# Attention as one pipeline of 24 rounds instead of six units one after another

## The chip, the cores and the metric

The kernel runs on one core of one Trainium2 chip. The metric is the device time of the program in microseconds (us). Five engines work beside each other, each in its own order: TensorE (PE, matmuls and transposes, with its weight loads shown as PEld), VectorE (DVE), ScalarE (ACT), GpSimd (POOL) and SyncE (SP), which issues the DMAs.

## The reference

One decoder layer on x (1024 tokens, width 1024). Its parts: a projection `z = rmsnorm(x) @ w_in`; a dilated attention branch and an RWKV-7 branch on parts of z; a gated merge of the two; a squared-ReLU MLP; a gated per-layer embedding. The change touches the attention branch alone:

```python
ATTN_GROUPS = ((128, 1), (512, 4), (2048, 16))    # (window, dilation), 4 heads of 64 each
q = rope(qkv[:, :, 0], pos); k = rope(qkv[:, :, 1], pos); v = qkv[:, :, 2]
for g, (window, dil) in enumerate(ATTN_GROUPS):
    idx = t[:, None] - dil * j[None, :]           # keys at stride dil, causal
    s = einsum('bqhd,bqjhd->bqhj', qb, kg) * scale
    m = max(s); e = exp(s - m); den = sum(e)
    o = einsum('bqhj,bqjhd->bqhd', e, vg) / den
# the three groups are combined per head by softmax over m + log(den)
```

## The kernel before

**Staging.** All activations stand transposed (features on partitions, tokens along the row). The program runs as: norm and transpose of x; the z projection, in items of 128 output features (48 matmuls of 128x512 into two PSUM banks, called z, half h = 0 and h = 1 with 24 each); RWKV's chunked scan among these items; attention among the last of them; merge, output projection, MLP, embedding.

**The order of the work.** The order of PE's instructions is written out by a planner at build time (class `Order`). It holds a list of dense items (`sch.add`: the z items and later work) and a set of chains (`sch.spawn`: generators for RWKV and attention). `run` takes a chain step whose planned time has come, and otherwise one more dense matmul (`fill`). The planned time of each step comes from fixed costs per engine (`Engine`, `Loads`, `HOP_DMA`, `LAG`), not from the chip. PE executes the list strictly in order. While attention runs, the order of the other engines is not the planner's: the language's own scheduler sets it.

**The units.** There are six attention units: three dilations in the order 16, 4, 1 (`GORD`), each with two pairs of heads. A unit has eight query blocks of 128 tokens. Unit n needs three z items in the order q, k, v (`add_attn`). Each half of q and k is copied out of PSUM by ScalarE (tile qk, permuted by dilation); behind the second half four DMAs build the swapped copy sw, GpSimd multiplies sw by the sine table, VectorE multiplies qk by the cosine table and adds sw (`turn_back`, rows sw and qk of the profile). v is copied out (tile v) and turned by eight PE transposes into vkb (`turn`, rows av). `attn_ok` says when the planner may take a unit's z items.

**One unit before.** `attention` waits until the unit's v is turned (`("vk", n) in done`), then until q and k are planned ready, and runs `unit`. That goes by pairs of blocks: `scores` (rows sc, into banks m0 and m1), masking and maximum on VectorE (rows SB, nm), exponentials on ScalarE (rows SB); then for each block of the pair before it the transposes of the weights (rows pt, banks s1 and s2), their copy PB on VectorE, and the values (rows po, bank s3), copied out on ScalarE to OTA or OTB. Each of these steps is handed to the planner apart, with a wait on the planned end of what it needs, so z matmuls stand between them. The next unit begins when the last block's values are issued; `natural` (rows rw, rc) turns the maxima and sums of a dilation at its end, and `combine` (rows cb) weighs the three dilations.

Of the kernel before, what the change touches and what calls it, by code (L numbers as in the profile page):

```python
# [10 lines left out]
F32 = mybir.dt.float32  # L11
F32R = mybir.dt.float32r
# [7 lines left out]
T = 1024  # L20
KT = D // 128
HD = 64
DILS = (1, 4, 16)
# [13 lines left out]
LEAD, SPARE, LAG = 0.4, 0.5, 0.4  # L37
# [204 lines left out]
def layer(ctx: ExitStack, tc: tile.TileContext, x, pT, wz, wup, w_out, wff1, w_ff2, w_ple, w_pleg,  # L242
# [3 lines left out]
    sch = Order()  # L246
# [21 lines left out]
    done = set()  # L268
# [31 lines left out]
    def wait(cond):  # L300
        while not cond():
            yield 0.1
# [603 lines left out]
    A = {}  # L906
    rope_t, MD, NAT = {}, {}, {}

    def attn_ok(n, x):
        if n < 2:  # L910
            return (("S", NU - 2) in done and ("E", NU - 1) in done and ("bv", NU - 1) in done
                    and (x < 2 or n == 0 or ("vk", 0) in done and ("v", NU - 1) in done))
        return ("B", n - 2) in done and (x < 2 or ("vk", n - 1) in done)

    def add_attn(n):
        gi, hp = n // 2, n % 2
# [51 lines left out]
    def attention():  # L968
        yield from wait(lambda: ("P", NU - 1, 1) in done)
        in_turn.__exit__(None, None, None)  # L970
        sch.in_turn = False
        V.shared = False
        amask = rtile([128, 384], "amask", "ex")
        SY.dma_start(amask, cst[:, C_BAND:C_BAND + 384])
        st = rtile([128, 512], "ast", "py")

        def stat(n=4):
            c = col[0]
            col[0] += 8 * n
            return st[:, c:c + 8 * n].rearrange("p (a b) -> p a b", b=n)  # L980

        SB = rtile([128, 4, 2, 256], "SB", "BK")
        PB = rtile([128, 4, 4, 128], "PB", "UV")
        vkb = rtile([128, 2, 8, 128], "vkb", "BT")

        def turn(n):
            yield from wait(lambda: 2 in A[n])
            yield sch.until(A[n]["t"])
            for b in range(2):
                ps, tag = yield from chain_bank([128, 4, 128], "av", ("s1", "s2"))  # L990
                for i in range(4):
# [3 lines left out]
            done.add(("vk", n))  # L995

        yield from turn(0)
        OTA = rtile([128, 2, 2, T], "OTA", "TM0")
        OTB = rtile([128, 2, 2, T], "OTB", "TM1")
        OT = {g: (OTA[:, 0], OTA[:, 1], OTB[:, 0])[i] for i, g in enumerate(GORD)}  # L1000
        for n in range(6):
            g, hp = GORD[n // 2], n % 2
            if hp == 0:
                MD[g] = stat(8)
            yield from wait(lambda: ("vk", n) in done)
            if n < 5:
                sch.spawn(turn(n + 1), 2)
            yield from wait(lambda: len(A[n].get("qk", ())) == 2)
            yield sch.until(max(A[n]["qk"]))
            if n == 5:  # L1010
                sraw = rtile([128, 768], "sraw", "v")
                SY.dma_start(sraw, cst[:, C_SEL:C_SEL + 768])
            yield from unit(n, g, hp, OT[g][:, hp], vkb[:, n % 2], SB, PB, amask)
            if n > 3:
                load_or(5 - n, G)
            if n == 5:
                load_or(2, G)
                load_or(3, V)
            if hp:
                NAT[g] = yield from natural(g, stat)  # L1020
        sel = rtile([128, 6, 128], "sel", "px", F32R)
        V.tensor_copy(sel.rearrange("p a b -> p (a b)"), sraw)
        yield from combine(OT, OTB[:, 1], stat, sel)

    def unit(n, g, hp, o, vk, SB, PB, amask):
        d = DILS[g]
        L = T // d
        q, k = A[n][0], A[n][1]
        band, bdm = amask[:, 0:256], amask[:, 256:384]
        B = {}  # L1030

        def scores(b0):
            yield from sch.free("m0", "m1")
            sps = [psum.tile([128, 2, 256], F32, name="sc", tag=f"m{h}") for h in range(2)]
            for b in (b0, b0 + 1):
                first = b % (L // 128) == 0 if L >= 128 else True
                w_ = 128 if first else 256
# [4 lines left out]
                B[b] = (first, w_, k0)  # L1042
            for b in (b0, b0 + 1):
                first, w_, k0 = B[b]
                sch.dep = sch.t
                msk = bdm if g == 2 else (band[:, 128:256] if first else band)
# [11 lines left out]
                B[b] = (e, w_ // 128, k0, sch.dep)  # L1058

        yield from scores(0)  # L1060
        for b0 in range(0, 8, 2):
            if b0 < 6:
                yield from scores(b0 + 2)
            for b in (b0, b0 + 1):
                e, nk, k0, t1 = B[b]
                yield sch.until(t1)
                tag = f"s{1 + b % 2}"
                yield from sch.free(tag)
                tp = psum.tile([128, 4, 128], F32, name="pt", tag=tag)
                for h in range(2):  # L1070
                    for j in range(nk):
                        tr(tp[:, 2 * h + j, :], e[:, h, j * 128:(j + 1) * 128], 0.107)
# [5 lines left out]
                sch.hold(tag)  # L1078
                B[b] = (P, nk, k0, sch.dep)
            for b in (b0, b0 + 1):  # L1080
                P, nk, k0, t1 = B[b]
                yield sch.until(t1)
                if b % 4 == 0:
                    yield from sch.free("s3")
                    po = psum.tile([128, 4, 128], F32, name="po", tag="s3")
                for j in range(nk):
                    for h in range(2):
                        hs = slice(64 * h, 64 * h + 64)
                        mm(po[hs, b % 4, :], vk[:, k0 // 128 + j, hs], P[:, 2 * h + j, :], 0.16,
                           start=j == 0, stop=j == nk - 1)  # L1090
            if b % 4 == 3:
                if d == 1:
                    dst, src = o[:, (b - 3) * 128:(b + 1) * 128], po.rearrange("p a b -> p (a b)")
                else:
                    nr = d // 2
                    r0 = (b // 4) * nr
                    dst = o.rearrange("p (i r) -> p r i", r=d)[:, r0:r0 + nr, :]
                    src = po.rearrange("p a b -> p (a b)").rearrange("p (r i) -> p r i", r=nr)
                S.activation(dst, src, AF.Copy)
                sch.hold("s3")  # L1100
        done.add(("B", n))

    def natural(g, stat):
        src = MD[g]
# [677 lines left out]
```

## Time and profile before

| | us |
|---|---|
| median of 3 runs | 1815.26 |
| lowest, highest | 1814.76, 1816.84 |
| the profiled execution | 1813.98 |
| its span | 1812.2 |
| PE busy | 1760.5 (97% of the span) |
| VectorE, ScalarE, GpSimd busy | 1046.7, 726.8, 769.0 |
| first av transpose, last cb matmul start | 538.1, 833.2 |

The page lists groups of instructions by source line. Since helpers issue nearly all of them, one line (L115, L271, L279) stands for many steps, and the tile's name tells which. A row such as `po<-PB,vkb` gives the tile written and those read. A plain fp32 matmul appears as two matmuls in the profile (x8 there is x4 in the order below). PE's busy rows overlap, so what an instruction costs is read from one start to the next. Timeline rows give the start, the duration, the engine, the operation and, in brackets, the idle time of the engine ahead of it and what ended it.

### The profile page before, as it was taken

The page shows a single profiled execution, that of the slowest core. Times are in us where ns is not written, and L with a number is a line of the kernel's source. Part 1 is how long each engine was busy: PE and PEld are TensorE (multiplying, and loading weights), DVE is VectorE, ACT ScalarE, POOL GpSimd, SP SyncE. Part 2 cuts the span into 40 slices and gives each one's busy share as a digit, 9 for nine tenths or more (in the row PEclk, how much of TensorE's full clock was granted, in tenths as well). Part 3 has the DMA queues.
Part 4 walks back from the last instruction along what each step waited for, and adds up shares of the span by engine and source line. Part 5 has one row for each costly group of instructions (what it writes and reads, how often), then busy time and mean ns, then how long its engine had stood idle before and what let it go on. Part 6 is the DMA issues. An engine that isn't in the chain of part 4 may idle for free.

```text
span 1812.2 us, 25836 instructions
## 1 busy us (share of the span) xinstructions
PE 1760.5 (97%) x10192; PEld 1430.0 (79%) x10192; DVE 1046.7 (58%) x1866; ACT 726.8 (40%) x1299; POOL 769.0 (42%) x507
## 2 busy tenths in 40 slices
PE   9999999999979999999999999999999999999898
PEld 8887777878766777777888788888888888887787
DVE  6289767676324233344745555556655577788454
ACT  5824423423324343452533533333333333334353
POOL 2344221231122322322230266666666797885421
PEclk9999989999999999999999999999999999999999
DMA  4621121213322222243633211112111111112221
GB/s 159 207 93 36 47 82 62 74 47 120 97 92 88 70 59 59 69 133 102 207 127 116 94 58 47 47 47 73 56 47 47 47 58 48 47 47 93 93 82 47
DMA packets 51546, 146.13 MB, mean 81 GB/s; under 512 B 6241, under 2 KB 6625, under 8 KB 51426
## 3 DMA queue, kind: packets, MB, share of 16 engines
q1 hardware_dynamic: 51426, 144.49, 24.3%
q8 instruction: 80, 1.31, 0.3%
q14 instruction: 40, 0.33, 0.1%
HBM read 110.52 MB, written 27.26 MB: 76 GB/s over the span
## 4 chain that ended last, share of the span: by engine, by line
PE 87%; DVE 6%; ACT 3%; issue 2%; DMA 1%; POOL 1%; SPq 0%; DVEq 0%; ACTq 0%; POOLq 0%
PE z L290 18%; PE z L292 18%; PE z L288 18%; PE bk L288 6%; PE bk L292 6%; PE bk L290 6%; PE po L271 1%; PE sc L271 1%; DVE tot L115 1%; DVE xy L115 1%; PE A L271 1%; PE y L271 1%; PE tp L279 1%; PE fq L271 1%; PE pt L279 1%
## 5 line engine op out<-in xcount | busy, mean ns | idle before, releaser
L115 DVE TENSOR_TENSOR tot<-tot,bk 128x512 f32<-128x512 f32 x468 | 308.0, 684 | 190.3 <-PE bk L292 189.6
L115 POOL TENSOR_TENSOR wl<-wr,wh 128x1024 fp32r<-128x1024 f32 (+1 forms) x88 | 212.2, 2411 | 476.8 <-ACT wh L115 476.8
L288 PE MATMUL z<-uh,wh 128*128 128x512 f32 (+1 forms) x800 | 315.4, 394 | 5.9 <-ACT part L115 3.0
L290 PE MATMUL z<-ul,wh 128*128 128x512 f32 (+1 forms) x800 | 317.6, 397 | 0.3 <-DVE ul L115 0.3
L292 PE MATMUL z<-uh,wl 128*128 128x512 f32 (+1 forms) x800 | 316.4, 396 | 1.1 <-POOL wl L115 1.1
L288 PE MATMUL z<-f,wh 128*128 128x512 f32 x512 | 200.0, 391 | 1.9 <-ACT f L115 1.9
L290 PE MATMUL z<-f,wh 128*128 128x512 f32 x512 | 199.9, 390 | 0.0
L292 PE MATMUL z<-f,wl 128*128 128x512 f32 x512 | 199.7, 390 | 0.0
L288 PEld LDWEIGHTS z<-uh,wh 128*128 128x128 f32 x800 | 151.8, 190 | 37.1 <-issue 4.9
L115 ACT ACTIVATE duo<-sum 128x512 fp32r<-128x512 f32 x150 | 90.3, 626 | 226.0 <-PE bk L292 109.6
L290 PEld LDWEIGHTS z<-ul,wh 128*128 128x128 f32 x800 | 152.0, 190 | 33.9 <-issue 7.9
L292 PEld LDWEIGHTS z<-uh,wl 128*128 128x128 f32 x800 | 152.1, 190 | 30.8 <-issue 3.9
L288 PE MATMUL bk<-duo 128*128 128x512 f32 x420 | 163.4, 389 | 0.0
L290 PE MATMUL bk<-duo 128*128 128x512 f32 x420 | 163.4, 389 | 0.0
L292 PE MATMUL bk<-duo 128*128 128x512 f32 x420 | 163.4, 389 | 0.0
L115 ACT ACTIVATE wh<-wr 128x1024 fp32r<-128x1024 f32 (+1 forms) x88 | 91.6, 1040 | 168.3 <-PE z L290 90.2
L115 POOL TENSOR_TENSOR duo<-sum,duo 128x512 fp32r<-128x512 f32 x75 | 100.6, 1341 | 102.4 <-ACT duo L115 102.4
L288 PEld LDWEIGHTS z<-f,wh 128*128 128x128 f32 x512 | 96.5, 189 | 22.1 <-ACT f L115 2.1
L290 PEld LDWEIGHTS z<-f,wh 128*128 128x128 f32 x512 | 96.5, 189 | 20.4 <-DVE f L115 0.4
L292 PEld LDWEIGHTS z<-f,wl 128*128 128x128 f32 x512 | 96.4, 188 | 19.9
L115 POOL TENSOR_TENSOR sum<-w2r 128x512 f32<-128x512 f32 x75 | 98.7, 1316 | 10.3 <-DMA oscr<-og 5.6
L115 POOL TENSOR_TENSOR sum<-hr 128x512 f32<-128x512 f32 x75 | 97.4, 1307 | 4.8 <-DVE duo L115 3.1
(302 smaller groups left out, 3190.2 us busy)
## 6 DMA issues: line engine op xcount, KB each, us to landing
wr<-in_wz_dram SPq DMA_DIRECT2D x48, 512.0 KB, 3.8
w2r<-in_w_ff_dram SPq DMA_DIRECT2D x32, 512.0 KB, 3.6
wr<-in_wff_dram SPq DMA_DIRECT2D x32, 512.0 KB, 3.5
xt<-in_x_dram SPq DMA_DIRECT2D x16, 512.0 KB, 4.3
gscr<-gst SPq DMA_DIRECT2D x32, 256.0 KB, 2.1
g<-gscr SPq DMA_DIRECT2D x16, 512.0 KB, 4.3
sw<-qk SPq DMA_DIRECT2D x48, 128.0 KB, 2.3
sascr<-lst SPq DMA_DIRECT2D x16, 256.0 KB, 4.5
```

The source lines that it names most:

```text
L115: return f(*a, **kw)
L271: PE.matmul(out_, a, b, start=start, stop=stop)
L279: PE.transpose(out_, a, ident if idn is None else idn)
L288: PE.matmul(ps, ah, bh, start=i == 0, stop=False)
L290: PE.matmul(ps, ah, bl, start=False, stop=False)
L292: PE.matmul(ps, al, bh, start=False, stop=i == n - 1)
```

## The change

`unit` is gone. All 24 pairs of blocks (6 units of 4) become rounds of one loop. Each pass waits until all five banks are planned free and then issues up to three pieces in one burst, without z matmuls between them: the values of round o, the transposes of round t, the scores of round s, where in steady state t is one round behind s and o one behind t. A unit's scores no longer wait for its v (only its values do), and they may begin while the unit before it is still in its last rounds. The v of unit n + 2 is turned when the values of unit n are issued. The z items of q and k of unit n + 2 are let go by the last scores of unit n (mark Q) and no longer by its last values (mark B); those of v by the turned v of unit n + 1 alone. `natural` becomes a chain of its own.

```diff
-        return ("B", n - 2) in done and (x < 2 or ("vk", n - 1) in done)
+        return (("Q", n - 2) if x < 2 else ("vk", n - 1)) in done
...
-        for n in range(6):
-            g, hp = GORD[n // 2], n % 2
-            if hp == 0:
+        def at_last(n):
+            yield from turn(n)
+            if n == 5:
+                sraw.append(rtile([128, 768], "sraw", "v"))
+                SY.dma_start(sraw[0], cst[:, C_SEL:C_SEL + 768])
...
+        sch.spawn(at_last(1), 2)
...
+        unit = lambda r: (r // 4, GORD[r // 8], r // 4 % 2)
+        blocks = lambda r: (2 * (r % 4), 2 * (r % 4) + 1)
+        s = t = o = 0
+        def scores(r):
...
-            yield from wait(lambda: ("vk", n) in done)
-            if n < 5:
-                sch.spawn(turn(n + 1), 2)
-            yield from wait(lambda: len(A[n].get("qk", ())) == 2)
-            yield sch.until(max(A[n]["qk"]))
...
-            yield from unit(n, g, hp, OT[g][:, hp], vkb[:, n % 2], SB, PB, amask)
-            if n > 3:
-                load_or(5 - n, G)
-            if n == 5:
-                load_or(2, G)
-                load_or(3, V)
-            if hp:
-                NAT[g] = yield from natural(g, stat)
...
+            if r % 4 == 3:
+                done.add(("Q", n))
+            if r % 8 == 7:
+                sch.spawn(nat(g), 2, 5.0)
+
+        def turns(r):
+            for b in blocks(r):
...
+        def values(r, po):
+            n, g, hp = unit(r)
...
+            if r % 4 == 3:
+                done.add(("B", n))
+                if n < 4:
+                    sch.spawn(at_last(n + 2), 2)
+                else:
+                    load_or(5 - n, G)
+
+        def asked(r):
+            return r < 24 and len(A[r // 4].get("qk", ())) == 2 and sch.t >= max(A[r // 4]["qk"]) + LAG
+
+        while o < 24:
+            yield from wait(lambda: (asked(s) or t < s or o < t) and (o == t or ("vk", o // 4) in done))
+            yield from sch.free("m0", "m1", "s1", "s2", "s3")
+            sch.dep = sch.t
+            at = s, t, o
+            if at[2] < at[1]:
+                if o % 2 == 0:
+                    po = psum.tile([128, 4, 128], F32, name="po", tag="s3")
+                values(o, po)
+                o += 1
+            if at[1] < at[0]:
+                turns(t)
+                t += 1
+            if asked(s):
+                scores(s)
+                s += 1
+            yield sch.until(sch.dep + 0.4)
+        load_or(2, G)
+        load_or(3, V)
+        yield from wait(lambda: len(NAT) == 3)
```

The bodies of `scores`, `turns` and `values` hold the same instructions as the three parts of `unit`.

PE, one round of a unit of dilation 1 (unit 4). Before:

```order
L271 MATMUL sc<-qk 128x256 x4
L290 MATMUL z<-ul_126,wh 128x512
L279 MATMUL pt<-cs,SB 128x128 x4
L292 MATMUL z<-uh_124,wl 128x512
L288 MATMUL z<-uh_124,wh 128x512
L279 MATMUL pt<-cs,SB 128x128 x4
L290 MATMUL z<-ul_126,wh 128x512
```

The same place with the change:

```order
L290 MATMUL z<-ul_125,wh 128x512
L292 MATMUL z<-uh_123,wl 128x512
L271 MATMUL po<-PB,vkb 64x128 x6
L279 MATMUL pt<-cs,SB 128x128 x8
L271 MATMUL sc<-qk 128x256 x4
L288 MATMUL z<-uh_123,wh 128x512
```

The transposes of both blocks stand together, with the values ahead of them and the scores behind, and 13 to 17 z matmuls stand between one burst and the next. From the first av to the last cb there are 123 runs of z matmuls before and 44 with the change; every PE instruction is there in both lists, and behind the last cb only the number of z ahead of the first merge matmul differs (81 before, 34 now).

PE, the start of unit 2 (round 8) in the changed order, with buffer numbers; z_5596 is the second half of unit 2's v item, and qk_5527 and qk_5458 are its k and q:

```order
L290 MATMUL z_5596<-ul1_126,wh_5498 128x512
L292 MATMUL z_5596<-uh1_124,wl_5499 128x512
L288 MATMUL z_5596<-uh1_124,wh_5498 128x512
L271 MATMUL sc_5607<-qk_5527,qk_5458 128x128
L271 MATMUL sc_5608<-qk_5527,qk_5458 128x128
```

These scores stand behind the first 10 of the 24 matmuls of z_5596. Before, they stood behind the whole v item, five more z, the eight av transposes and two z. ScalarE shows the same place (v_5594 is v, its halves from z_5569 and z_5596). Before:

```order
L115 ACTIVATE qk_5527<-z_5529 128x128x4
L115 ACTIVATE v_5594<-z_5569 128x128x4
L115 ACTIVATE wh_5624<-wr_5622 128x1024
L115 ACTIVATE v_5594<-z_5596 128x128x4
L115 ACTIVATE vkb_4918<-av_5634 128x512
L115 ACTIVATE vkb_4918<-av_5640 128x512
L115 ACTIVATE SB_4916,ast_4915<-SB_4916,nm_5656 128x128 x2
```

With the change:

```order
L115 ACTIVATE qk_5527<-z_5529 128x128x4
L115 ACTIVATE v_5594<-z_5569 128x128x4
L115 ACTIVATE SB_4916,ast_4915<-SB_4916,nm_5615 128x128 x2
L115 ACTIVATE SB_4916,ast_4915<-SB_4916,nm_5621 128x256 x2
L115 ACTIVATE wh_5642<-wr_5640 128x1024
L115 ACTIVATE v_5594<-z_5596 128x128x4
```

The exponentials of the unit's first round (SB) stand between the two halves of v. Units 3, 4 and 5 begin in the same way, with their first scores behind 10 of the 24 matmuls of the second half of v.

More of the change, by code (lines that the diff above doesn't have):

```diff
@@ L995, in turn, with nat @@
             done.add(("vk", n))
+        def at_last(n):
[3 more added lines that the diff above has]
+                SY.dma_start(sraw[0], cst[:, C_SEL:C_SEL + 768])
+        def nat(g):
+            NAT[g] = yield from natural(g, stat)
+        sraw = []
         yield from turn(0)
+        sch.spawn(at_last(1), 2)
         OTA = rtile([128, 2, 2, T], "OTA", "TM0")
@@ L1000, in attention @@
         OT = {g: (OTA[:, 0], OTA[:, 1], OTB[:, 0])[i] for i, g in enumerate(GORD)}
-        for n in range(6):
-            g, hp = GORD[n // 2], n % 2
-            if hp == 0:
-                MD[g] = stat(8)
-            yield from wait(lambda: ("vk", n) in done)
-            if n < 5:
-                sch.spawn(turn(n + 1), 2)
-            yield from wait(lambda: len(A[n].get("qk", ())) == 2)
-            yield sch.until(max(A[n]["qk"]))
-            if n == 5:
-                sraw = rtile([128, 768], "sraw", "v")
-                SY.dma_start(sraw, cst[:, C_SEL:C_SEL + 768])
-            yield from unit(n, g, hp, OT[g][:, hp], vkb[:, n % 2], SB, PB, amask)
-            if n > 3:
-                load_or(5 - n, G)
-            if n == 5:
-                load_or(2, G)
-                load_or(3, V)
-            if hp:
-                NAT[g] = yield from natural(g, stat)
[L1021 to L1033, printed above, removed]
+        unit = lambda r: (r // 4, GORD[r // 8], r // 4 % 2)
+        blocks = lambda r: (2 * (r % 4), 2 * (r % 4) + 1)
+        s = t = o = 0
+        B = {}
+        po = None
+        def scores(r):
+            n, g, hp = unit(r)
+            per = T // DILS[g] // 128
+            if r % 8 == 0:
+                MD[g] = stat(8)
+            q, k = A[n][0], A[n][1]
             sps = [psum.tile([128, 2, 256], F32, name="sc", tag=f"m{h}") for h in range(2)]
-            for b in (b0, b0 + 1):
-                first = b % (L // 128) == 0 if L >= 128 else True
-                w_ = 128 if first else 256
+            for b in blocks(r):
+                w_ = 128 if b % max(per, 1) == 0 else 256
                 k0 = (b + 1) * 128 - w_
@@ L1041, in scores @@
                     mm(sps[h][:, b % 2, :w_], q[hs, b * 128:(b + 1) * 128], k[hs, k0:k0 + w_], w_ / 750)
[L1042 to L1046, printed above, removed]
+                B[r, b] = (w_, k0)
+            for b in blocks(r):
+                w_, k0 = B[r, b]
+                msk = amask[:, 256:384] if g == 2 else amask[:, 256 - w_:256]
                 e = SB[:, b % 4]
@@ L1057, in scores @@
                                  accum_out=MD[g][:, b, 4 + 2 * hp + h:5 + 2 * hp + h])
[L1058 to L1069, printed above, removed]
+            if r % 4 == 3:
[3 more added lines that the diff above has]
+        def turns(r):
+            for b in blocks(r):
+                nk = B[r, b][0] // 128
+                tp = psum.tile([128, 4, 128], F32, name="pt", tag=f"s{1 + b % 2}")
                 for h in range(2):
                     for j in range(nk):
-                        tr(tp[:, 2 * h + j, :], e[:, h, j * 128:(j + 1) * 128], 0.107)
+                        tr(tp[:, 2 * h + j, :], SB[:, b % 4, h, j * 128:(j + 1) * 128], 0.107)
                 P = PB[:, b % 4]
@@ L1077, in unit @@
                     V.tensor_copy(P[:, 0::2, :], tp[:, 0::2, :])
[L1078 to L1085, printed above, removed]
+                sch.hold(f"s{1 + b % 2}")
+        def values(r, po):
+            n, g, hp = unit(r)
+            d = DILS[g]
+            vk, out_ = vkb[:, n % 2], OT[g][:, hp]
+            for b in blocks(r):
+                w_, k0 = B.pop((r, b))
+                nk = w_ // 128
                 for j in range(nk):
@@ L1088, in unit @@
                         hs = slice(64 * h, 64 * h + 64)
[L1089 removed]
+                        mm(po[hs, b % 4, :], vk[:, k0 // 128 + j, hs], PB[:, b % 4, 2 * h + j, :], 0.16,
                            start=j == 0, stop=j == nk - 1)
[L1091 removed]
+            if r % 2:
+                b = 2 * (r % 4)
+                src = po.rearrange("p a b -> p (a b)")
                 if d == 1:
[L1093 removed]
+                    dst = out_[:, (b - 2) * 128:(b + 2) * 128]
                 else:
@@ L1096, in unit @@
                     r0 = (b // 4) * nr
-                    dst = o.rearrange("p (i r) -> p r i", r=d)[:, r0:r0 + nr, :]
-                    src = po.rearrange("p a b -> p (a b)").rearrange("p (r i) -> p r i", r=nr)
+                    dst = out_.rearrange("p (i r) -> p r i", r=d)[:, r0:r0 + nr, :]
+                    src = src.rearrange("p (r i) -> p r i", r=nr)
                 S.activation(dst, src, AF.Copy)
                 sch.hold("s3")
-        done.add(("B", n))
+            if r % 4 == 3:
[26 more added lines that the diff above has]
+        yield from wait(lambda: len(NAT) == 3)
+        sel = rtile([128, 6, 128], "sel", "px", F32R)
+        V.tensor_copy(sel.rearrange("p a b -> p (a b)"), sraw[0])
+        yield from combine(OT, OTB[:, 1], stat, sel)
     def natural(g, stat):
```

## The prediction

> **What bounds the kernel now.** I read the page first, then the stretch that the change touches, then its waits, and last single rounds in the timeline.
>
> ```profile
> PE 1760.5 (97%) x10192; PEld 1430.0 (79%) x10192; DVE 1046.7 (58%) x1866; ACT 726.8 (40%) x1299; POOL 769.0 (42%) x507
> PE 87%; DVE 6%; ACT 3%; issue 2%; DMA 1%; POOL 1%; SPq 0%; DVEq 0%; ACTq 0%; POOLq 0%
> ```
>
> TensorE (PE) is busy 97% of the span and carries 87% of the chain that ended last. The attention rounds stand between 542 and 836 us; for that stretch the view by windows gives (columns: stretch, its length, then busy time of PE, weight loads, VectorE, ScalarE and GpSimd, then the granted clock):
>
> ```profile
> 542.00:836.00 294.00, 290.02 (x1600) 215.01 (x1599) 110.88 (x353) 123.82 (x288) 87.25 (x37) 1.00 0.27 80
> ```
>
> PE is idle for 4.0 us of 294 and at full clock. No other engine is over half busy. So the change can win in two ways only: PE's own instructions must take less time from start to start, or the 4 us of waits must go. It loses one for one if PE, which works in order, is made to wait. The waits there (who waited, for whom, total us, times, longest):
>
> ```profile
> PE av L279 <- ACT v L115: 2.1, 3, 0.8
> PE po L271 <- DVE PB L115: 1.1, 1, 1.1
> PE sc L271 <- DVE yc L115: 0.6, 1, 0.6
> ```
>
> **The gain: fewer excursions.** A busy row of PE overlaps the next, so cost is read from start to start. One steady round at dilation 1 (the profile counts each plain fp32 matmul twice):
>
> ```profile
> 739.47 1.13 PE L271 MATMUL sc<-qk 64*128 64x256 f32 x8
> 740.54 0.50 PE L290 MATMUL z<-ul,wh 128*128 128x512 f32 x1
> 740.87 0.60 PE L279 MATMUL pt<-cs,SB 128*128 128x128 f32 x4
> 741.23 0.48 PE L292 MATMUL z<-uh,wl 128*128 128x512 f32 x1
> 741.54 0.40 PE L288 MATMUL z<-uh,wh 128*128 128x512 f32 x1
> 741.78 0.60 PE L279 MATMUL pt<-cs,SB 128*128 128x128 f32 x4
> 742.14 0.47 PE L290 MATMUL z<-ul,wh 128*128 128x512 f32 x1
> 742.45 0.39 PE L292 MATMUL z<-uh,wl 128*128 128x512 f32 x1
> 742.68 0.40 PE L288 MATMUL z<-uh,wh 128*128 128x512 f32 x1
> ...
> 743.47 0.66 PE L271 MATMUL po<-PB,vkb 128*64 128x128 f32 x8
> 744.05 0.49 PE L288 MATMUL z<-uh,wh 128*128 128x512 f32 x1
> 744.48 0.66 PE L271 MATMUL po<-PB,vkb 128*64 128x128 f32 x8
> 745.07 0.49 PE L271 MATMUL sc<-qk 64*128 64x256 f32 x2
> ```
>
> The round lasts 745.07 − 739.47 = 5.60 us. It holds nine z matmuls (two lie in the cut), and one z to the next is 742.68 − 742.45 = 0.23, or 2.04 for nine. The other 3.56 us are attention. It leaves the z stream four times (scores with the values before them, two transposes, the other values).
>
> In the changed order a round is one burst: values, transposes, scores. From the same rows: the two po groups take 743.47 to 744.05 = 0.58 and 744.48 to 745.07 = 0.59. How much of that is entering and leaving a short group shows at dilation 16:
>
> ```profile
> 560.37 0.38 PE L279 MATMUL pt<-cs,SB 128*128 128x128 f32 x2
> 560.50 0.47 PE L288 MATMUL z<-uh,wh 128*128 128x512 f32 x1
> ...
> 563.10 0.44 PE L271 MATMUL po<-PB,vkb 128*64 128x128 f32 x4
> 563.47 0.71 PE L271 MATMUL sc<-qk 64*128 64x128 f32 x8
> ```
>
> Four po rows take 0.37, eight 0.59, so each four add 0.22: sixteen together cost 0.59 + 0.44 = 1.03. Two pt rows take 0.13, four 0.36, so eight cost 0.80. Scores cost 740.54 − 739.47 = 1.07. Passing from pt to sc is in no row; pt to z costs 0.03 and po to sc 0.20 beyond the last start, so it adds between 0 and 0.17, and since both neighbours differ in rows used, as po and sc differ from z, I take 0.17. Entering and leaving from z: now 0.10 (sc to pt) + 0.08 to 0.10 (pt to pt) + 0.20 (742.14 to 743.47, less five z) + 0.20 (po to po) = 0.59; then one run from sc to po, 0.20. Together 1.03 + 0.80 + 0.17 + 1.07 + 0.20 = 3.27 against 3.56: **0.29 us a round**, for three excursions less, 0.10 each. The lists of PE's rows have 123 runs of z from the first av to the last cb before and 44 after: 79 × 0.10 = 7.9. The short bursts at a unit's ends save more than that, since a lone sc or po pays 0.2 at each side, which makes at most 79 × 0.13 = 10. I take **−9.0 us**, between 7.9 and 10.
>
> **The gain: the av waits.** Now the value transposes (av) stand five z behind the end of the v item; in the change av comes behind a whole burst, at dilation 4 and 1 two z, then pt and sc, some 2 us behind v, against five z (1.1) and the wait (0.7) now. **−2.1 us**, at worst 0. The 1.1 us wait of po I leave as it is: 0, at best −1.1.
>
> **The loss: scores that stand ahead of their keys.** In units 2 to 5 the first scores now wait behind av, which waits for the second half of v. The change drops that, and its order puts the first scores inside the last half of the v item: 34 z behind the end of the k item, 14 z ahead of the end of v. What must happen between k's last z and the first scores, for unit 2 (ScalarE, SyncE, GpSimd, VectorE, ScalarE):
>
> ```profile
> 621.71 1.06 ACT L115 ACTIVATE wh<-wr 128x1024 fp32r<-128x1024 f32 x1 [4.15 <-PE z L290]
> 622.67 1.09 ACT L115 ACTIVATE qk<-z 128x512 f32<-128x512 f32 x1
> 623.79 2.42 SPq L128 DMA_DIRECT2D sw<-qk  x4
> 628.10 3.44 POOL L115 TENSOR_TENSOR sw<-sw,rope 128x1024 f32<-128x1024 f32 x1 [2.85 <-DMA sw<-qk]
> 631.57 1.23 DVE L115 TENSOR_TENSOR qk<-qk,sw 128x1024 f32<-128x1024 f32 x1 [2.28 <-POOL sw L115]
> 632.59 1.06 ACT L115 ACTIVATE wh<-wr 128x1024 fp32r<-128x1024 f32 x1 [4.15 <-PE z L290]
> ```
>
> The weight split wh of 621.71 is let go by the last z of k, that of 632.59 by the last z of v. The keys are turned at 631.57 + 1.23 = 632.80, 11.1 us behind k and 0.2 behind v; 34 z are only 7.7 us. The scores reach PE's head 14 × 0.227 = 3.2, less 0.1 for the change of form, before 632.57, at 629.5: PE waits 632.84 − 629.5 = 3.35 us. Nothing hides it: the z behind the scores are queued behind them. Units 3, 4 and 5 (keys turned, v's end):
>
> ```profile
> 678.11 1.23 DVE L115 TENSOR_TENSOR qk<-qk,sw 128x1024 f32<-128x1024 f32 x1 [2.29 <-POOL sw L115]
> 679.14 1.06 ACT L115 ACTIVATE wh<-wr 128x1024 fp32r<-128x1024 f32 x1 [4.10 <-PE z L290]
> 725.91 1.22 DVE L115 TENSOR_TENSOR qk<-qk,sw 128x1024 f32<-128x1024 f32 x1 [2.28 <-POOL sw L115]
> 727.34 1.06 ACT L115 ACTIVATE wh<-wr 128x1024 fp32r<-128x1024 f32 x1 [4.61 <-PE z L290]
> 774.62 1.23 DVE L115 TENSOR_TENSOR qk<-qk,sw 128x1024 f32<-128x1024 f32 x1 [2.29 <-POOL sw L115]
> 776.17 1.06 ACT L115 ACTIVATE wh<-wr 128x1024 fp32r<-128x1024 f32 x1 [4.66 <-PE z L290]
> ```
>
> Keys against v's end: +0.2, −0.2, −0.3, so waits of 3.35, 2.95 and 2.8. Together **+12.4 us**. The work ahead of these places (z alone for 50 z and more) is the same, so I see no way for the keys to come sooner. Unit 1's keys are turned long before; unit 0 starts as now.
>
> **The loss behind the loss: the clock.** PE's clock halves after some waits and not after others:
>
> ```profile
> 225.03:228.44 3.41, 1.43 (x7) 0.88 (x6) 2.05 (x4) 3.08 (x4) 2.28 (x1) 1.00 0.00 0
> 228.45:231.86 3.41, 3.41 (x9) 2.64 (x9) 0.91 (x4) 0.00 (x0) 0.08 (x1) 0.50 0.89 306
> 532.23:535.64 3.41, 1.59 (x7) 0.94 (x5) 0.00 (x0) 0.41 (x1) 0.00 (x0) 1.00 0.95 281
> 535.65:539.06 3.41, 1.67 (x13) 1.54 (x14) 2.59 (x2) 2.47 (x5) 2.70 (x2) 1.00 0.56 198
> ```
>
> A wait of 1.98 us that fell whole into one stretch of 3.41 left PE busy 1.43 there, and the next 3.41 ran at 0.50: 1.7 us lost. A wait of some 3.6 us that two stretches shared (busy 1.59 and 1.67) cost no clock. So the clock goes when a stretch has under about 1.5 us of work, which a wait of 3.35 brings about in nine places of ten and one of 2.8 in seven of ten. That is 3.3 of the four; with three, and 1.7 to 3 us each (one stretch, or a second where the first half-clock stretch begins idle), I take 3 × 2.2 = **+6.6 us**, between 0 and 12.
>
> The Trainium skill ("TensorE: Matmul & The Clock Gate", What's actually happening) lets the clock fall "after ≥1 idle window (~3.4µs)". By that rule none of the four waits, all under 3.41, would cost clock, and the sum would be 6.6 us lower; the trace here disagrees, with a half clock behind 1.98 us.
>
> **Other waits.** All five banks must be planned free before a burst, and pt waits for its exponentials. The slowest round now: sc ends at 740.6, the exponentials (four ScalarE rows) at 744.4:
>
> ```profile
> 743.88 0.49 ACT L115 ACTIVATE SB<-SB,nm 128x256 f32<-128x256 f32 x1
> ```
>
> That is 3.8 us; the burst's gap of 17 z (3.9) and the po ahead of pt (1.0) hide it with 1 us to spare, less what GpSimd or a weight split holds up. I take +0.5, between 0 and 3.
>
> **Sum**: −9.0 − 2.1 + 12.4 + 6.6 + 0.5 = +8.4. The profiled execution took 1813.98 (span 1812.2 and 1.8 around it), 1.3 under the median of the runs, so 1822.4 in its terms and **1823.7 us** against the median of 1815.26. PE's order behind the combine is the same row for row, so nothing is won or lost there.
>
> **Rivals.** (a) The clock holds: the four waits come, but each is shared by two stretches, as the one at 535. For it: that row. Against: four waits would have to fall so. 1823.7 − 6.6 = 1817.1. (b) The keys are in time, because the order ahead of the scores leaves them longer than I read, and the change does what it says: −9.0 − 2.1 + 0.5 = −10.6, **1804.7**. It decides if the keys take under 7.7 us from k's end; against it stand the four chains above, 10.6 to 11.1 us each (k's end is v's end less 48 z, 10.9 us). (c) Every burst waits for exponentials as well: half a us in 24 bursts, +12, 1835.7; for it the 1 us to spare, against it the whole exponentials' time that 17 z cover.
>
> **Chances**: forecast 0.58, (a) 0.20, (b) 0.14, (c) 0.08. A measurement of this kernel tells 0.2% (3.6 us) from no change. (b) is faster, with a little of (a): 0.15; (a) is within, 0.20; the rest slower, 0.65. The range leaves out (b) and the upper part of (c): 1811 to 1831.
>
> **What would show it.** Right: four waits "PE sc <- DVE qk" of 2.8 to 3.4 us, one ahead of each unit from the third on; half-clock stretches behind most of them; no "PE av <- ACT v"; and dilation-1 bursts of some 3.3 us beside their z. Wrong: scores of those units that start without idle time, or waits at pt spread over all bursts.

## The result, and the profile after

The changed kernel takes 1827.70 us (median of 9 runs, 1820.20 to 1832.75) against 1814.76 for the kernel before (9 runs beside them): a ratio of 1.0076, 95% interval 1.0056 to 1.0096. It is slower, by 12.9 us where 8.4 were forecast (1823.7, range 1811 to 1831). Its profiled execution took 1823.96 (span 1822.2), 10.0 us more than that of before.

The page of the changed kernel, busy time of the engines:

```profile
PE 1759.1 (97%) x10192; PEld 1437.3 (79%) x10192; DVE 1051.8 (58%) x1866; ACT 726.3 (40%) x1299; POOL 768.8 (42%) x507
```

PE's busy time is 1.4 us less than before although the span is 10.0 us longer, so by the page the time went into idle PE (what a half clock costs hides in the busy time). The waits of PE from 538 to 860 us name it (who waited, for whom, total us, times, longest):

```profile
PE sc L271 <- DVE qk L115: 12.4, 4, 3.5
PE po L271 <- DVE PB L115: 2.5, 1, 2.5
PE pt L279 <- ACT SB L115: 0.2, 1, 0.2
```

The av waits and the wait of sc for yc are gone. So is the 1.1 us wait of po for PB, which stood at 738 us. In their place the scores wait for their keys four times, and the values once, at 811 us, for the weights' copy PB. PE's timeline shows the four places, at the head of units 2, 3, 4 and 5 (in brackets the idle time and what ended it):

```profile
627.61 1.55 PE L271 MATMUL sc<-qk 64*128 64x128 f32 x8 [3.50 <-DVE qk L115]
...
676.86 0.93 PE L271 MATMUL sc<-qk 64*128 64x128 f32 x8 [3.23 <-DVE qk L115]
...
725.77 0.93 PE L271 MATMUL sc<-qk 64*128 64x128 f32 x8 [2.97 <-DVE qk L115]
...
776.51 0.93 PE L271 MATMUL sc<-qk 64*128 64x128 f32 x8 [2.75 <-DVE qk L115]
```

The view by windows, cut along the 3.41 us stretches of the clock, shows what came behind them (length, busy time of PE, weight loads, VectorE, ScalarE, GpSimd, granted clock):

```profile
624.35:627.76 3.41, 0.15 (x2) 0.15 (x4) 1.23 (x1) 0.00 (x0) 1.95 (x1) 1.00 0.00 0
627.77:631.18 3.41, 3.41 (x13) 2.37 (x14) 1.40 (x10) 0.68 (x3) 0.00 (x0) 0.50 0.01 2
...
672.14:675.55 3.41, 1.49 (x7) 0.91 (x5) 1.19 (x1) 0.43 (x1) 3.40 (x1) 1.00 0.33 133
675.56:678.97 3.41, 2.12 (x13) 1.57 (x14) 2.38 (x10) 0.00 (x0) 0.00 (x0) 1.00 0.00 0
...
726.75:730.16 3.41, 3.41 (x9) 2.64 (x10) 1.35 (x10) 1.86 (x8) 0.00 (x0) 0.50 0.00 0
...
777.92:781.33 3.41, 3.41 (x10) 2.63 (x9) 0.95 (x8) 1.60 (x2) 0.00 (x0) 0.50 0.31 125
```

Three of the four waits were followed by a half-clock stretch. The wait that ended at 676.86 fell across two stretches (PE busy 1.49 and 2.12) and cost no clock. A steady burst of dilation 1:

```profile
796.76 0.39 PE L290 MATMUL z<-ul,wh 128*128 128x512 f32 x1
797.08 1.09 PE L271 MATMUL po<-PB,vkb 128*64 128x128 f32 x16
798.10 1.09 PE L279 MATMUL pt<-cs,SB 128*128 128x128 f32 x8
799.13 1.14 PE L271 MATMUL sc<-qk 64*128 64x256 f32 x8
800.19 0.50 PE L292 MATMUL z<-uh,wl 128*128 128x512 f32 x1
800.53 0.39 PE L288 MATMUL z<-uh,wh 128*128 128x512 f32 x1
```

From the z ahead of it to the second z behind are 3.77 us; less two z of 0.23 the burst costs 3.31, against 3.56 for a round before.

**Where the 10.0 us lie.** From the first av to the first transpose of the merged output PE does the same work in every version. The window over that part, in the order before, after (length first, then PE's busy time):

```profile
538.35:975.65 437.30, 433.18 (x2232) 333.05 (x2231) 177.34 (x444) 175.88 (x369) 122.29 (x52) 1.00 0.31 99
```

```profile
537.35:984.84 447.49, 431.78 (x2233) 340.69 (x2232) 179.71 (x444) 175.27 (x369) 121.03 (x51) 0.98 0.31 96
```

It is 10.2 us longer; ahead of it the changed kernel is 1.0 shorter, behind it 0.8 longer. I split this part three ways: idle time of PE (gaps of 0.08 us and more between its rows); half of PE's working time inside half-clock stretches, as an estimate of what the clock cost; and the rest, PE's work at full clock. The experiments below are split alike.

| from the first av to the merge, us | length | idle | lost to the clock | rest | runs of z |
|---|---|---|---|---|---|
| before | 437.3 | 4.0 | 0 | 433.3 | 123 |
| after | 447.5 | 15.6 | 7.7 | 424.2 | 44 |
| late scores | 428.9 | 3.0 | 0 | 426.0 | 45 |
| half as late | 431.6 | 5.8 | 1.1 | 424.6 | 44 |
| late scores, bursts split | 429.8 | 2.0 | 1.6 | 426.2 | 80 |
| before, blocks joined in pairs | 433.4 | 7.4 | 1.7 | 424.3 | 75 |
| keys on VectorE from unit 2 | 443.0 | 13.7 | 4.6 | 424.7 | 44 |
| weight split on VectorE | 446.7 | 13.2 | 8.5 | 425.0 | 44 |

So the change did win 9.1 us on PE, and paid 11.6 in idle time and 7.7 in clock. Two cautions. The versions with whole bursts (after, late scores, half as late, the last two rows) have a rest of 424.2 to 426.0, so the gain on PE is known to some 2 us only: 7.3 in late scores, where no half clock blurs it. And a part of the clock's loss stands at the head of this window, behind the last wait of RWKV (yt, some 3.5 us), which the change does not touch: 0.8 after, 1.1 in half as late, 1.6 with bursts split, 1.7 with blocks joined, 1.2 and 1.7 in the last two rows. What is left behind waits of the attention itself is 6.8 after (four stretches of 1.7), 3.4 with the keys on VectorE, 6.8 with the weight split, and 0 in the others.

### The profile page after: what moved, and what is told of

It reads as the page before. It is cut to its first block, busy times and chain, and to the rows that moved or that the text cites. A ratio compares the mean times of both kernels' runs of the same rounds, so it can differ in the third digit from the quotient of the medians.

```text
span 1822.2 us, 25834 instructions
## 1 busy us (share of the span) xinstructions
PE 1759.1 (97%) x10192; PEld 1437.3 (79%) x10192; DVE 1051.8 (58%) x1866; ACT 726.3 (40%) x1299; POOL 768.8 (42%) x507
## 4 chain that ended last, share of the span: by engine, by line
PE 54%; DVE 2%; ACT 1%; DMA 1%; issue 1%; POOL 0%; SPq 0%; DVEq 0%; ACTq 0%; POOLq 0%
PE z L290 11%; PE z L292 11%; PE z L288 11%; PE bk L288 6%; PE bk L292 6%; PE bk L290 6%; DVE tot L115 1%; DMA g<-gscr 1%; PE tp L279 1%; PE sc L271 0%; PE po L271 0%; PE pt L279 0%; DVE mt L115 0%; DMA wr<-in_w_out_dram 0%; DVE ast L115 0%
```

## The experiments

**Scores held back.** Theory: the loss is the four waits and the clock behind them, so first scores that stand behind their keys give the gain without the loss.

```diff
-            return r < 24 and len(A[r // 4].get("qk", ())) == 2 and sch.t >= max(A[r // 4]["qk"]) + LAG
+            return r < 24 and len(A[r // 4].get("qk", ())) == 2 and sch.t >= max(A[r // 4]["qk"]) + LAG + (3.8 if r > 7 and r % 4 == 0 else 0.0)
```

In PE's list the first scores of unit 2 move 17 z back, those of units 3 and 4 as many, those of unit 5 by 34.

> The changed kernel with one edit: the first scores of units 2 to 5 are planned 3.8 us later than the planned end of their keys. Theory (PE waits 12.4 us for the turned keys, and its clock halves behind those waits): the four waits and the half-clock stretches behind them go, the gain of the bursts stays; against the kernel before -8.9 (switches) -0.6 (yc) -0.6 (av, which now follows v closely, about 0.5 us a unit) +1.4 and +1.7 (the wait of po for PB near the end and its clock) = about -7 us, 1808 us, ratio 0.996. Rival (the bursts themselves cost the time, by exponentials and banks): about the changed kernel's time, ratio 1.005 to 1.008.

Measured: 1803.96 us, ratio 0.9943, interval 0.9924 to 0.9962: faster than both kernels. PE's waits from 536 to 860 us are now

```profile
PE yt L279 <- ACT rb L115: 3.5, 1, 3.5
PE pt L279 <- ACT SB L115: 1.1, 2, 1.0
PE sc L271 <- DVE yc L115: 0.6, 1, 0.6
```

and the first scores of unit 2 start without idle time behind their keys (turned at 628.20 + 1.23):

```profile
628.20 1.23 DVE L115 TENSOR_TENSOR qk<-qk,sw 128x1024 f32<-128x1024 f32 x1 [2.29 <-POOL sw L115]
...
629.97 0.93 PE L271 MATMUL sc<-qk 64*128 64x128 f32 x8
```

The theory stands. What I had not foreseen is that the wait for PB went as well; the run with the weight split says why. (The yt row is RWKV's last wait, just ahead of the first av; it stands in the kernel before too, and where it falls between windows differs.)

**Half as late.** The same edit with 1.8 in place of 3.8, to see whether the clock hangs on the length of the wait.

> As the run with 3.8 us, but 1.8 us later: units 2 to 4 should wait 1.7, 1.4 and 1.2 us, unit 5, which the order moves further, not at all: 4.3 us of waits, each too short to halve the clock. Theory (waits and clock): against the kernel before -8.9 -2.1 -0.6 +4.3 +1.4 +1.7 = -4 us, 1811 us, ratio 0.998, no half-clock stretch at the units' starts. Rival (only the length of the waits counts, the clock costs nothing): 8.1 us of waits less than the changed kernel, so about +5 us against before, 1820 us, ratio 1.003.

Measured: 1808.77, ratio 0.9979, interval 0.9963 to 0.9995.

```profile
PE sc L271 <- DVE qk L115: 4.6, 4, 1.5
```

The four waits are still there, at 1.5 us and less (0.45 in unit 5, where I expected none), and no half-clock stretch follows any of them in the profile. Of the 12.4 us of waits 4.6 are left, and the median is 18.9 us below the changed kernel's: 7.8 are shorter waits, 2.5 the PB wait, which is gone here too, and the 8.6 that remain I put down to the clock (mean granted clock of the runs 0.988, against 0.983 in the changed kernel). The rival, that the clock costs nothing, falls: 1820, or 1817.5 with the PB wait taken off, lies above what was measured.

**Keys sooner, first try.** The other way to mend the waits is to shorten the chain of the keys. The sine product goes from GpSimd (3.39 to 3.45 us) to VectorE, and the scores are held by 1.2 more, so that the first scores of units 2 to 5 stay behind the same z matmul as in the changed kernel.

```diff
-            G.tensor_tensor(sw, sw, rope_t[g][:, 1], OP.mult)
+            V.tensor_tensor(sw, sw, rope_t[g][:, 1], OP.mult)
```

> The changed kernel with the sine product of the keys moved from GpSimd (3.4 us) to VectorE (1.2 us behind the cosine product), the first scores of units 2 to 5 kept at the same z matmul as in the changed kernel. Theory (PE waits there for the turned keys): the keys come about 1.0 us sooner and the four waits shrink by as much, 12.4 to about 8.3 us; two half-clock stretches instead of three; 4 to 8 us faster than the changed kernel, ratio to before 1.003 to 1.005. Rival (the waits come from something else, as ScalarE's exponentials or a bank): the waits stay at 2.7 to 3.5 us and the ratio at 1.0075.

Measured: 1807.49, ratio 0.9954, interval 0.9940 to 0.9968, far below what I expected. The waits did as foreseen:

```profile
PE sc L271 <- DVE qk L115: 8.4, 4, 2.7
PE po L271 <- DVE PB L115: 2.7, 1, 2.7
```

and no half clock stood behind them in this profile, where two stretches of the clock shared each wait. But that makes only some 12 to 14 us of the 20 (4.0 of waits, and the 8 to 10 of clock). The edit has a second effect that I had overlooked: the planner's costs for units 0 and 1 change with it, and PE's order differs from 155 rows ahead of the first av on. The next two runs separate the two.

**The same edit in the kernel before.**

> The kernel before with the sine product on VectorE alone, where no scores stand ahead of their keys. In the profile with that edit in the changed kernel, the waits of PE ahead of the attention had shrunk (q for AR from 8.2 to 0.9 us, yt from 4.2 to 0.7), since the edit moves the planner's order there (PE's first different row is 155 rows ahead of the first av). If that is where most of the gain came from, the kernel before gains it too: 1815.8 - 8 = 1808, ratio 0.9955. Rival: the gain lies in the keys, and the kernel before, which never waited for them, gains nothing: 1.000.

Measured: 1806.21, ratio 0.9963, interval 0.9946 to 0.9980. The kernel before, which never waited for its keys, gains nearly as much. PE's waits ahead of the attention, before and with the edit:

```profile
PE q L271 <- DVE AR L115: 8.2, 3, 5.6
PE yt L279 <- ACT rb L115: 4.5, 2, 3.6
```

```profile
PE q L271 <- DVE AR L115: 0.9, 1, 0.9
PE yt L279 <- ACT rb L115: 0.8, 1, 0.8
```

So some 10 us of that run came from RWKV's last steps, which had been waiting in both kernels, and not from the change studied here.

**Keys sooner from unit 2 on.** With the product on VectorE only where `n > 1`, PE's order up to the first scores of unit 2 is that of the changed kernel row for row. The scores are held by 1.2, as in the first try.

```diff
-            G.tensor_tensor(sw, sw, rope_t[g][:, 1], OP.mult)
+            (V if n > 1 else G).tensor_tensor(sw, sw, rope_t[g][:, 1], OP.mult)
```

> The changed kernel with the sine product on VectorE from unit 2 on only, so that the order up to the first scores of unit 2 is that of the changed kernel row for row. The keys come some 1.1 us sooner, so the four waits shrink from 12.4 to some 8.4 us and stay under 2.8 us: -4, and with them most of the half clock behind them (of the 20 us at half clock that the granted clock of the changed kernel's runs shows over that of before, some 14, so -7). From 1827.7: 1817, ratio 1.001. Rival: the clock does not hang on these waits, -4 alone: 1824, ratio 1.0053.

Measured: 1817.22, ratio 1.0014, interval 1.0000 to 1.0029, as the theory had it; the rival's 1.0053 lies outside. The mean granted clock of the ten runs is 0.987, against 0.983 in the changed kernel. The waits are 2.42, 2.13, 1.86 and 1.64 us; they end at 630.30, 678.50, 727.90 and 775.98. Cut along the stretches of the clock in this trace (the stretch of the wait and the one behind it, for the first three):

```profile
PE sc L271 <- DVE qk L115: 8.0, 4, 2.4
```

```profile
628.43:631.84 3.41, 1.54 (x11) 1.11 (x12) 2.37 (x7) 0.00 (x0) 0.00 (x0) 1.00 0.00 0
631.85:635.26 3.41, 3.41 (x10) 2.63 (x9) 0.81 (x8) 1.86 (x8) 0.00 (x0) 0.50 0.01 2
676.21:679.62 3.41, 1.28 (x10) 0.79 (x10) 2.37 (x3) 0.00 (x0) 0.00 (x0) 1.00 0.01 4
679.63:683.04 3.41, 3.41 (x9) 2.63 (x9) 1.24 (x10) 1.86 (x8) 0.00 (x0) 0.50 0.00 0
724.00:727.41 3.41, 2.04 (x9) 1.34 (x8) 3.24 (x3) 0.47 (x1) 0.00 (x0) 1.00 0.32 131
727.42:730.83 3.41, 2.93 (x17) 2.26 (x18) 1.74 (x11) 0.69 (x3) 0.00 (x0) 1.00 0.00 0
```

Half clock followed the two waits of over 2 us, each inside one stretch. The wait of 1.86 was shared by two stretches and cost no clock, so this trace does not show what a wait of that length costs inside one.

**Bursts split again.** With late scores, one z matmul was put between the pieces of each burst, to price an excursion by itself.

```diff
                 values(o, po)
                 o += 1
+                yield 0.1
             if at[1] < at[0]:
                 turns(t)
                 t += 1
+                yield 0.1
```

> As the run with 3.8 us, with one z matmul put between the pieces of each burst (values, transposes, scores): 36 more runs of z, the pipeline itself as it is. Theory (each excursion from the z stream costs 0.10 to 0.13 us of entering and leaving): 3.6 to 4.7 us slower than the run with 3.8 us, about -3 us against before, ratio 0.998. Rival (the switches are free, the whole gain comes from waits removed): the same time as the run with 3.8 us.

Measured: 1806.61, ratio 0.9963, interval 0.9947 to 0.9980: 2.6 us above late scores, with overlapping intervals. The table is clearer than the times: with 35 more runs of z the rest grows by 0.2 us, and not by the 3.5 that 0.10 each would make. Leaving the z stream between values, transposes and scores costs next to nothing more than passing straight from one to the next.

**Blocks joined in pairs, in the kernel before.** The opposite edit: only the transposes of both blocks of a pair are put together, and the values of both; units, scores and keys stay as they were.

```diff
+            yield sch.until(max(B[b0][3], B[b0 + 1][3]))
+            yield from sch.free("s1", "s2")
             for b in (b0, b0 + 1):
                 e, nk, k0, t1 = B[b]
-                yield sch.until(t1)
                 tag = f"s{1 + b % 2}"
-                yield from sch.free(tag)
...
+            yield sch.until(max(B[b0][3], B[b0 + 1][3]))
+            if b0 % 4 == 0:
+                yield from sch.free("s3")
             for b in (b0, b0 + 1):
                 P, nk, k0, t1 = B[b]
-                yield sch.until(t1)
                 if b % 4 == 0:
-                    yield from sch.free("s3")
```

> The kernel before with one part of the change alone: in each round the transposes of both blocks are issued together, and so are the values of both; units, their start behind av, and scores stay as they are. 123 runs of z become 75. Theory after the split-burst run (most of the gain lies in joining the two halves of a round, some 0.15 us for each run of z that goes): 48 x 0.15 = 7 us faster than before, ratio 0.996, PE's waits as before (4 us), no half clock at the units' starts. Rival (the gain lies in joining values, transposes and scores): 48 x 0.06 = 3 us at most, ratio 0.998.

Measured: 1811.44, ratio 0.9974, interval 0.9963 to 0.9985. The time lies between theory and rival; the profile decides. The rest falls by 9.0 us with 48 fewer runs of z (0.19 each on average), as much as in the changed kernel with 79 fewer. So all or nearly all of PE's gain comes from joining the like halves (pt with pt, po with po), and the round's three kinds in one burst add nothing that shows. More than half of it is lost again in this version: idle +3.4, most of it a 3.0 us wait of the last values for PB, and clock +1.7, which stands not there but behind RWKV's last wait.

**The weight split.** That wait stands in the changed kernel as well. VectorE, GpSimd and PE around it, in the changed kernel's timeline (rows of other tiles left out):

```profile
805.57 2.40 POOL L115 TENSOR_TENSOR wl<-wr,wh 128x1024 fp32r<-128x1024 f32 x1 [10.41 <-ACT wh L115]
805.70 4.68 DVE L115 TENSOR_TENSOR ast<-ast 128x32 f32<-128x32 f32 x3 [2.88 <-ACT ast L115]
...
807.93 2.40 POOL L115 TENSOR_TENSOR orw<-wr,orw 128x1024 fp32r<-128x1024 f32 x1
...
810.30 1.27 DVE L115 COPY PB<-pt 128x512 f32<-128x512 f32 x2
...
811.03 1.33 PE L271 MATMUL po<-PB,vkb 128*64 128x128 f32 x16 [2.54 <-DVE PB L115]
```

Three small statistics of the combine (`ast`) take 4.68 us and hold up the PB copies queued behind them, exactly while GpSimd runs two splits. A first try put the split of orw on VectorE in the version with late scores:

```diff
-                    load_or(5 - n, G)
+                    load_or(5 - n, V)
...
-        load_or(2, G)
+        load_or(2, V)
```

> As the run with 3.8 us, with the splits of the three RWKV outputs that GpSimd made (orw) moved to VectorE. Theory (the wait of po for PB at the end comes from VectorE's small statistics, which stand still while GpSimd splits): that wait shrinks from 2.5 us to under 0.5 and its half clock goes, 3 to 4 us faster than the run with 3.8 us, about -10.5 us against before, ratio 0.994. Rival (that wait comes from VectorE's order alone): the same as the run with 3.8 us or 1 us slower.

Measured: 1807.41, ratio 0.9963, interval 0.9950 to 0.9975: no faster than late scores alone, a miss. There was nothing to gain there: in late scores the combine's statistics meet an idle GpSimd (0.97 us for five of them) and the PB wait is gone already.

```profile
799.13 0.97 DVE L115 TENSOR_TENSOR ast<-ast 128x32 f32<-128x32 f32 x5 [1.46 <-ACT ast L115]
...
802.49 2.39 POOL L115 TENSOR_TENSOR orw<-wr,orw 128x1024 fp32r<-128x1024 f32 x1 [13.97 <-ACT orw L115]
```

The same edit in the changed kernel itself, where the wait is:

> The changed kernel with the split of the output projection's weights (orw) on VectorE and not on GpSimd; PE's order up to the last values stays as it is. Theory: the 2.54 us wait of the last values for PB came because three small statistics on VectorE stood still (4.68 us) through two GpSimd splits, wl and orw, 2.40 us each. With orw gone from GpSimd they are held through wl alone, some 2.4 us sooner, and the wait shrinks to 0 to 0.3 us, with no half clock behind it: 1827.7 - 2.4 - 1.7 = 1823.6, ratio 1.0055. Rival: the three rows are slow for another reason (what they read, or the ScalarE copy beside them): they stay above 4 us, the wait stays 2.5 us, and the time with it: ratio 1.0076. The profile tells them apart; the times differ by about what a measurement can tell.

Measured: 1824.38, ratio 1.0055, interval 1.0037 to 1.0073.

```profile
810.59 2.39 POOL L115 TENSOR_TENSOR wl<-wr,wh 128x1024 fp32r<-128x1024 f32 x1 [18.48 <-ACT wh L115]
810.67 2.69 DVE L115 TENSOR_TENSOR ast<-ast 128x32 f32<-128x32 f32 x3 [2.88 <-ACT ast L115]
...
814.01 1.26 PE L271 MATMUL po<-PB,vkb 128*64 128x128 f32 x16 [0.45 <-DVE PB L115]
```

With one split on GpSimd instead of two, the three statistics take 2.69 instead of 4.68 and the wait is 0.45 instead of 2.54, with no half clock behind it. The profile shows the mechanism; the gain in time it does not, since the two times' intervals overlap. The four waits of the scores are as before (12.2 us), and in this profile all four were followed by half clock, where in the changed kernel's profile three were. The Trainium skill ("SBUF — State Buffer", Who interferes with whom) says that a VectorE instruction with two inputs in SBUF contends with a GpSimd instruction that reads SBUF. The trace agrees: 0.97 us for five such rows beside an idle GpSimd, 2.69 for three beside one split, 4.68 beside two.

**Both mends together.** The sine product on VectorE for all units, and the first scores held by 5.0 in place of 1.2: 16 z matmuls later than in the changed kernel at units 2 to 4, 34 at unit 5.

> The sine product on VectorE, as in the run before it, and the first scores of units 2 to 5 put 16 z matmuls later, as in the run with late scores. If the two gains are separate, this takes off the four waits for the keys that the sine product on VectorE left (8.4 us) and the 2.7 us wait for the last PB: 1807.5 - 8.4 - 2.7 = 1796.4, ratio 0.989. Rival: what the product on VectorE gained was only that waits went, so that with late scores nothing is left for it: 1804, ratio 0.994.

Measured: 1797.14, ratio 0.9909, interval 0.9893 to 0.9925, the best version. The two gains add: PE waits for no key, and RWKV's last steps no longer wait either.

```profile
PE pt L279 <- ACT SB L115: 1.7, 2, 0.9
PE av L279 <- ACT v L115: 1.5, 3, 0.8
PE rc L279 <- DVE row L115: 0.6, 1, 0.6
```

## Why the prediction was right

The sign and the mechanism held: four waits, and half clock behind most of them. The time came 4.5 us further out than forecast. By its steps:

- **Switches, −9.0: measured −9.1** (433.3 to 424.2), −7.3 in late scores. The sum was about right by luck, since its working was not. I priced each excursion alike, at 0.10 to 0.13; in fact nearly all of it lies in the joined halves, about 0.19 for each of 48, and the other 31 of the 79 are nearly free. A burst of dilation 1 came to 3.31 where I had 3.27: 1.02 for po, 1.03 for pt with the passage to sc (I had 0.97), 1.06 for sc, 0.20 for entering and leaving.
- **The av waits, −2.1: right**; the row is gone.
- **Scores ahead of their keys, +12.4: measured +12.4**, as 3.50, 3.23, 2.97 and 2.75 against 3.35, 3.35, 2.95 and 2.8. Counting z matmuls from the end of k in the order, and reading the key chain from the trace, gave this to within 0.15 us each.
- **The clock, +6.6: 7.7 in the profile, more in the median.** Three of the four waits were followed by half clock, as counted, and cost 5.1 us; a fourth stretch behind the PB wait cost 1.7, and the end of one behind RWKV's last wait, at 535, made the rest. In the weight split's profile all four waits were followed by half clock: 6.8. So for the waits that it named, the term was about right. The clock as a whole lost more. The profiled execution was one of the milder: its mean granted clock is 0.986, that of the nine runs 0.983 on average, that of the kernel before 0.989 (29 runs beside late scores). From these, half-clock time is 2 × (1 − 0.9827) × 1825.9 (the median's span) = 63 us in the mean run against 2 × (1 − 0.9886) × 1812.2 = 41, so up to 11 us are lost, and not 6.6. This difference would make most of the distance from 1823.7 to 1827.7. Four waits of the scores and the PB wait at 1.7 each would make 8.5 of it; where the remaining 2.5 stand, no trace shows. In late scores the mean clock is 0.988 again, so most of the added half clock goes with the waits.
- **Other waits, +0.5, and 0 for po: together about +1.3.** The 1.1 us wait of po for PB, which I had left as it is, went, and another of 2.5 came at the last values; the wait of sc for yc (0.6) went, pt waits 0.2 once, a matmul behind the combine (bk) 0.5, and smaller gaps shrank by 0.2. I had not asked what the wait for PB was. Before, too, it came behind a VectorE row that ran long while GpSimd split a weight: nm took 2.05 us there, and 0.16 at 796.03 with GpSimd idle.

```profile
735.30 2.37 POOL L115 TENSOR_TENSOR orw<-wr,orw 128x1024 fp32r<-128x1024 f32 x1 [4.46 <-ACT orw L115]
735.65 2.05 DVE L115 TENSOR_SCALAR nm<-ast 128x2 f32<-128x2 f32 x1
737.62 0.41 DVE L115 COPY PB<-pt 128x256 f32<-128x256 f32 x1
```

  With the change two splits met the statistics of the combine.

Of the rivals, (a) the clock that holds is refuted by the three half-clock stretches; (b) keys in time by the four waits, though late scores shows that its price was near: −10.6 forecast, −10.0 measured once the scores stand late enough; (c) by 0.2 us of waits at pt.

The rule of the Trainium skill that I weighed ("TensorE: Matmul & The Clock Gate", What's actually happening), half clock after an idle window of about 3.4 us, would have made 6.6 us less; here half clock followed waits of 2.13 and 2.42 us (keys on VectorE from unit 2). The trace decides against it.

## What to carry to other kernels

When an order is rewritten to save switches, first list what each moved instruction needs and count the distance on the path that makes it: here 34 matmuls (7.7 us) stood where the keys take 11.1, and an in-order engine paid the difference with its clock on top, while holding the scores back by 17 matmuls turned a loss of 0.8% into a gain of 0.6%. Join like instructions first; joining unlike ones into a longer burst brought nothing that showed here. A wait of 2.1 to 2.4 us on TensorE cost 1.7 more in clock here when it fell into one stretch, and waits of 1.5 us and less cost none, so shortening such waits pays before removing them does.

## What the runs showed of the hardware

- In each trace the half clock starts and ends on a grid of 3.41 us, and in the attention it hung on how much TensorE worked within one stretch of that grid. Stretches with 0.15, 0.97, 1.43 and 1.04 us of work (after) and with 1.28 and 1.54 (keys on VectorE from unit 2) were followed by half clock; stretches with 1.49 (after) and 2.04 (keys on VectorE from unit 2) were not. So the bound lies near 1.5 us in these traces and is not sharp.
- Where a wait falls among these stretches differs from run to run: the same four waits were followed by half clock three times after and four times with the weight split. The nine runs of the changed kernel spread over 12.6 us, and their granted clock goes from 0.987 in the fastest to 0.980 in the slowest, which is about as much (0.007 × 1826 = 12.8). The kernel before spreads over 9.9, so this is not the change's alone.
- Busy time is not the whole rule. In the last version a stretch with 1.68 us of work was followed by half clock:

```profile
763.43:766.84 3.41, 1.68 (x8) 0.76 (x6) 2.61 (x6) 1.85 (x9) 0.98 (x1) 1.00 0.23 50
766.84:770.25 3.41, 3.38 (x13) 1.98 (x12) 1.17 (x4) 3.37 (x5) 0.00 (x0) 0.50 0.50 190
```

  About 0.9 us of that work were transposes (pt). The Trainium skill ("TensorE: Matmul & The Clock Gate", Part 4: PE-mode transpose) says that transposes do not count as busy in the same way; by that rule some 0.7 us counted, and this stretch would fit; so would one in the late version with the weight split (770.93 to 774.34: 2.03 us, 1.38 of it transposes, half clock behind it). Another goes against it: the stretch from 535.65 to 539.06 before, with 1.67 us of which 1.36 were transposes (yt and av), was not followed by half clock. And in late scores, ahead of the attention, the stretch from 451.12 to 454.53, with 3.14 us of work and none of it transposes, was followed by half clock; 2.18 us of that work were 64 matmuls of 32x32 (tq). What else the clock counts stays open.
- On TensorE, passing from values to transposes to scores directly costs as much as with one z in between: with one z between the pieces, 35 more runs of z cost 0.2 us in all.
